# A block of two layers in float32: the low part of every fourth weight unit, made by an adding transfer instead of a VectorE subtraction

## The chip, the core and the metric

The kernel runs on one core of a Trainium2 chip. The metric is the device time of one execution in microseconds (us). A core has five engines with instruction queues of their own: TensorE (PE, matrix products; its weight loads are listed as PEld), VectorE (DVE), ScalarE (ACT), GpSimd (POOL) and SyncE (SP, which here only issues transfers). Each queue is worked off in order; engines wait for each other by semaphores. Transfers between HBM and SBUF run on 16 DMA engines beside all that; they can be issued from the queues of SP, ACT and POOL.

## What is computed

The reference takes x (256 tokens by 2048) through two layers, each a mixer and an MLP, with a root-mean-square norm ahead and a residual sum behind each:

```python
for layer in range(DEPTH):                     # DEPTH = 2
    j = layer // 2
    if layer % 2 == 0:
        y = s5_hgrn2_layer(rms_norm(h, even_norm[j]), even_w_in[j], ...)
    else:
        y = attention_layer(rms_norm(h, odd_norm[j]), odd_w_qkv[j], ...)
    h = h + y
    h = h + squared_relu_mlp(rms_norm(h, mlp_norm[layer]), mlp_w_up[layer], mlp_w_down[layer])
```

The first mixer is a state-space scan and a gated recurrence side by side, the second attention over a sliding window. An MLP is `square(relu(x @ w_up)) @ w_down` with 8192 hidden columns. Nearly all of the work is products of 256 tokens with weights: 2048x5120, 1024x1024 and 2048x2048 in the first mixer, 2048x2560 and 2048x2048 in the second, 2048x8192 and 8192x2048 in each MLP. All of it is float32.

## The kernel before, in words

**Products in parts.** TensorE is fed with float32r, a rounded form of float32. To keep float32's precision, each operand is split into a high part (the value rounded to float32r) and a low part (value minus high part), and three products are summed: high x high, high x low and low x high. The activations are kept as such pairs (class `Pair`), and every weight is split on its way in.

**Units.** All weights are cut, in the order of their use, into 704 units of 512 KB: 128 partitions by 1024 float32, as `nk` row blocks of 128 by `1024 // nk` columns (two blocks of 512 columns; four of 256 for the MLP's up product). In order: 80 units of the first projection, 8 of a gate, 32 of the first output product, 256 of the first MLP, 40 and 32 of the attention, 256 of the second MLP. For each unit:

- `emit_dma` (L92 to L98) issues the load into a tile `raw` from SP's queue (L97). There are four raw tiles.
- `emit_split` (L100 to L107) makes the high part `whi` by an ACT copy that rounds (L105), and the low part `wlo` by a DVE subtraction, raw minus high (L106). There are four tiles of each. Only unit 0 is handled in two pieces.
- `wblock`, `ublock` and `xblock` (L138 to L185) use the unit: 12 to 24 products through the helper `mm` (L136), of which a third read `wlo`. They gather a block of the result in PSUM over several units. In `xblock` the weights are the moving operand, in the other two the stationary one.

**How far ahead.** `advance` (L109 to L119) is called by the blocks for each unit: before unit i is used, the loads up to unit i + 6 and the splits up to unit i + 3 are emitted, a load never more than four units ahead of the splits. So a split must wait until the unit before last has left its tiles, and a load until the raw tile of four units ago has been read.

**Other work.** The mixers are generators put on a list `side`; after each unit `pump` lets them emit a little. They use all engines. On POOL's queue lie, before the change, only some memsets, small powers for the norms (L348, L770, L878, L984), small loads at the start and the load of h (L847).

**Order.** The order of the instructions in each queue is settled when the kernel is built: a scheduler takes the emitted instructions by priority, times them in a simulation of its own, and gives tiles to buffers as it goes (`schedule_with_timeline_sim=True`). Semaphore waits follow from which instruction reads or writes which tile. The MLP's stages run up, up, down, up, down, up, down, down over quarters of the hidden columns (L931 to L938).

Of the kernel before, what the change touches and what calls it, by code (L numbers as in the profile page):

```python
# [8 lines left out]
F32 = mybir.dt.float32  # L9
# [4 lines left out]
AF = mybir.ActivationFunctionType  # L14
ALU = mybir.AluOpType
# [45 lines left out]
def hybrid_kernel(ctx: ExitStack, tc: tile.TileContext, x, even_norm, even_w_in, s5_lambda_re, s5_lambda_im,  # L61
                  s5_log_dt, s5_b_re, s5_b_im, s5_c_re, s5_c_im, s5_d, s5_w_glu, s5_b_glu, hgrn_lower_bound,
                  hgrn_o_norm, even_w_out, odd_norm, odd_w_qkv, q_norm, k_norm, att_sinks, odd_w_out,
                  mlp_norm, mlp_w_up, mlp_w_down, cfd, cmd, out, stop=None):
    nc = tc.nc
    V, S, G, PE = nc.vector, nc.scalar, nc.gpsimd, nc.tensor
# [20 lines left out]
    def pieces(i):  # L87

        nk = units[i][3]
        return [slice(k, k + 1) for k in range(nk)] if i == 0 else [slice(0, nk)]  # L90
# [9 lines left out]
    def emit_split(i):  # L100
        raw, nk = raws.pop(i), units[i][3]
        hi = wp.tile([P, nk, 1024 // nk], F32R, tag="whi", name="whi")
        lo = wp.tile([P, nk, 1024 // nk], F32R, tag="wlo", name="wlo")
        for ks in pieces(i):
            S.copy(out=hi[:, ks], in_=raw[:, ks])  # L105
            V.tensor_tensor(out=lo[:, ks], in0=raw[:, ks], in1=hi[:, ks].bitcast(F32), op=ALU.subtract)  # L106
        splits[i] = (hi, lo)  # L107

    def advance():  # L109
        i = ptr["use"]  # L110
        while ptr["dma"] < min(len(units), i + LOOK_DMA + 1) or ptr["split"] < min(len(units), i + LOOK + 1):
            if ptr["dma"] < min(len(units), i + LOOK_DMA + 1) and ptr["dma"] < ptr["split"] + 4:
                emit_dma(ptr["dma"])
                ptr["dma"] += 1
            else:
                emit_split(ptr["split"])
                ptr["split"] += 1
        ptr["use"] += 1
        return splits.pop(i)  # L119
# [193 lines left out]
    for q in range(8):  # L313
        lastx = make_xT(xt, XT0, "g0", 2 * q, 2)
        if q == 0:
            with tc.issue_after(lastx[2].ins):
                for _ in range(REWARM):
                    PE.matmul(wps, warm[:, 0:P], warm, start=True, stop=True, skip_group_check=True)
        if q < 4:
            emit_split(ptr["split"])  # L320
            ptr["split"] += 1
            if q < 3:
                emit_dma(ptr["dma"])
                ptr["dma"] += 1
                load_x(5 + q)
# [818 lines left out]
```

## Time and profile before

| | |
|---|---|
| median of 3 runs | 2093.21 us (2092.36 to 2093.96) |
| the profiled execution | 2093.33 us, of which the span of the program's instructions 2091.4 us |
| mean granted TensorE clock | 0.998 of full speed |
| the two MLPs, from the timeline | about 410 to 1130 us and 1383 to 2091 us |
| HBM read and written | 374.75 MB and 2.10 MB |
| transfers issued from POOL's queue (q0) | 672 packets, 2.15 MB |

How to read it: a row of instructions names the source line, engine, operation and tiles (written <- read), then the count, the busy time and the mean duration, then the idle time of the engine ahead of them and what ended it. A row of the waits names who waited for whom, the total in us, how often, and the longest. A row of the timeline has the start and the duration first. A row of transfers has the queue that issues them, their count and size, and the median time from issue to landing. "acc" is a block's sum in PSUM, "chi" and "clo" the pair of the MLP's hidden activations (and scratch elsewhere), "x" the pair of a norm's output, "h" the residual stream, "m" the mixers' PSUM tiles.

### The profile page before, as it was taken

The page shows a single profiled execution, that of the slowest core. Times are in us where ns is not written, and L with a number is a line of the kernel's source. Part 1 is how long each engine was busy: PE and PEld are TensorE (multiplying, and loading weights), DVE is VectorE, ACT ScalarE, POOL GpSimd, SP SyncE. Part 2 cuts the span into 40 slices and gives each one's busy share as a digit, 9 for nine tenths or more (in the row PEclk, how much of TensorE's full clock was granted, in tenths as well). Part 3 has the DMA queues.
Part 4 walks back from the last instruction along what each step waited for, and adds up shares of the span by engine and source line. Part 5 has one row for each costly group of instructions (what it writes and reads, how often), then busy time and mean ns, then how long its engine had stood idle before and what let it go on. Part 6 is the DMA issues. An engine that isn't in the chain of part 4 may idle for free.

```text
span 2091.4 us, 30709 instructions
## 1 busy us (share of the span) xinstructions
PE 2077.8 (99%) x12208; PEld 1771.9 (85%) x12208; DVE 1319.9 (63%) x1794; ACT 1036.9 (50%) x1385; POOL 37.8 (2%) x38
## 2 busy tenths in 40 slices
PE   9999999999999999999999999999999999999999
PEld 8988988888888888888888888788888888888887
DVE  6799967666655565565555688776564555565554
ACT  5877555454443444444344477554443444344332
POOL 2000000000000000000000110000000000000000
PEclk9999999999999999999999999999999999999999
DMA  8454644556655665665555643466665665665564
GB/s 247 121 152 142 210 151 163 177 177 188 190 191 193 191 190 191 193 190 191 192 190 183 190 149 125 140 181 187 188 190 193 192 190 192 193 190 191 192 205 147
DMA packets 263968, 378.86 MB, mean 181 GB/s; under 512 B 14120, under 2 KB 147792, under 8 KB 263504
## 3 DMA queue, kind: packets, MB, share of 16 engines
q1 hardware_dynamic: 262400, 373.62, 56.9%
q8 instruction: 96, 1.57, 0.3%
q0 software_dynamic: 672, 2.15, 0.3%
q10 hardware_dynamic: 752, 1.12, 0.2%
q14 instruction: 48, 0.39, 0.1%
HBM read 374.75 MB, written 2.10 MB: 180 GB/s over the span
## 4 chain that ended last, share of the span: by engine, by line
PE 97%; DMA 1%; ACT 1%; DVE 0%; issue 0%; DVEq 0%; SPq 0%; ACTq 0%
PE acc L136 92%; PE m L136 4%; DMA raw<-in_even_w_in_dram 1%; PE m L1037 1%; PE m L304 1%; ACT whi L105 0%; PE m L400 0%; PE m L1071 0%; ACT chi L530 0%; PE m L777 0%; DVE wlo L106 0%; DVE t L343 0%; PE m L537 0%; PE m L509 0%; ACT L832 0%
## 5 line engine op out<-in xcount | busy, mean ns | idle before, releaser
L106 DVE TENSOR_TENSOR wlo<-raw,whi 128x1024 fp32r<-128x1024 f32 (+1 forms) x705 | 860.8, 1222 | 685.4 <-ACT whi L105 684.8
L105 ACT CAST whi<-raw 128x1024 fp32r<-128x1024 f32 (+1 forms) x705 | 740.5, 1051 | 964.6 <-PE acc L136 838.9
L136 PE MATMUL acc<-x,whi 128*128 128x512 f32 (+1 forms) x2944 | 811.1, 362 | 2.5 <-ACT x L843 2.4
L136 PEld LDWEIGHTS acc<-x,wlo 128*128 128x128 f32 x2496 | 470.5, 189 | 92.1 <-DVE wlo L106 0.9
L136 PE MATMUL acc<-x,wlo 128*128 128x256 f32 x2496 | 530.5, 279 | 0.7 <-DVE wlo L106 0.7
L136 PE MATMUL acc<-whi,chi 128*128 128x512 f32 x1280 | 499.6, 390 | 0.0
L136 PE MATMUL acc<-whi,clo 128*128 128x512 f32 x1280 | 499.2, 390 | 0.0
L136 PE MATMUL acc<-wlo,chi 128*128 128x512 f32 x1280 | 498.6, 390 | 0.0
L136 PEld LDWEIGHTS acc<-x,whi 128*128 128x128 f32 x2944 | 453.9, 190 | 4.8 <-ACT x L843 2.8
L136 PEld LDWEIGHTS acc<-whi,chi 128*128 128x128 f32 x1280 | 240.3, 188 | 50.3 <-issue 0.8
L136 PEld LDWEIGHTS acc<-whi,clo 128*128 128x128 f32 x1280 | 240.3, 188 | 49.3
L136 PEld LDWEIGHTS acc<-wlo,chi 128*128 128x128 f32 x1280 | 240.3, 188 | 49.1
L136 PE MATMUL acc<-whi,x 128*128 128x512 f32 x576 | 181.5, 393 | 0.0
L136 PEld LDWEIGHTS acc<-whi,x 128*128 128x128 f32 x576 | 107.5, 188 | 22.4 <-issue 0.4
L136 PE MATMUL acc<-wlo,x 128*128 128x512 f32 x288 | 113.3, 394 | 0.0
L136 PEld LDWEIGHTS acc<-wlo,x 128*128 128x128 f32 x288 | 54.1, 188 | 10.8 <-issue 0.2
L926 DVE SCALAR_TENSOR_TENSOR h<-acc,rs2g,h 128x512 f32<-128x512 f32 x64 | 45.1, 747 | 21.3 <-PE acc L136 21.3
L912 DVE SCALAR_TENSOR_TENSOR t<-t 128x512 f32<-128x512 f32 x64 | 44.3, 693 | 2.2
L911 DVE TENSOR_TENSOR t<-acc,t 128x512 f32<-128x512 f32 x64 | 43.8, 684 | 0.0
L915 DVE TENSOR_TENSOR clo<-t,chi 128x512 fp32r<-128x512 f32 x64 | 43.8, 684 | 0.0
L914 ACT CAST chi<-t 128x512 fp32r<-128x512 f32 x64 | 39.4, 616 | 0.0
L910 ACT COPY t<-acc 128x512 f32<-128x512 f32 x64 | 37.1, 579 | 0.0
(213 smaller groups left out, 899.9 us busy)
## 6 DMA issues: line engine op xcount, KB each, us to landing
raw<-in_mlp_w_up_dram SPq DMA_DIRECT2D x256, 512.0 KB, 3.7
raw<-in_mlp_w_down_dram SPq DMA_DIRECT2D x256, 512.0 KB, 3.6
raw<-in_even_w_in_dram SPq DMA_DIRECT2D x79, 512.0 KB, 3.9
raw<-in_odd_w_qkv_dram SPq DMA_DIRECT2D x40, 512.0 KB, 3.7
raw<-in_even_w_out_dram SPq DMA_DIRECT2D x32, 512.0 KB, 3.6
raw<-in_odd_w_out_dram SPq DMA_DIRECT2D x32, 512.0 KB, 3.7
raw<-in_s_w_glu_dram SPq DMA_DIRECT2D x8, 512.0 KB, 3.5
xt<-in_x_dram SPq DMA_DIRECT2D x8, 256.0 KB, 8.0
```

The source lines that it names most:

```text
L105: S.copy(out=hi[:, ks], in_=raw[:, ks])
L106: V.tensor_tensor(out=lo[:, ks], in0=raw[:, ks], in1=hi[:, ks].bitcast(F32), op=ALU.subtract)
L136: PE.matmul(o, a, b, start=start, stop=stop, skip_group_check=True, **kw)
L304: ipe = PE.transpose(ps[:, b, t * P:(t + 1) * P], src[:, t, (a + b) * P:(a + b + 1) * P], ident)
L910: S.copy(out=r, in_=acc[:, :, 1])
L911: V.tensor_tensor(out=r, in0=acc[:, :, 0], in1=r, op=ALU.add)
L912: V.scalar_tensor_tensor(out=r, in0=r, scalar=0.0, in1=r, op0=ALU.max, op1=ALU.mult)
L914: S.copy(out=ch[c].hi[:, ks, :], in_=r)
L915: V.tensor_tensor(out=ch[c].lo[:, ks, :], in0=r, in1=ch[c].hi[:, ks, :].bitcast(F32), op=ALU.subtract)
L926: V.scalar_tensor_tensor(out=h[:, t, cs], in0=acc[:, t], scalar=norm.rs2[:, t:t + 1], in1=h[:, t, cs], op0=ALU.mult, op1=ALU.add)
L1037: PE.transpose(ps[:, r, a, :], pr[:, 2 * a + r, k * P:(k + 1) * P], ident)
```

## The change

For every unit i with i % 4 == 3 and i > 11 the DVE subtraction is left out. A second ACT pass writes the negated high part into `lo`, and a transfer issued from POOL's queue adds the raw weights to what stands in `lo`. The result is again raw minus high. All other units are split as before.

```diff
         for ks in pieces(i):
             S.copy(out=hi[:, ks], in_=raw[:, ks])
+            if i % 4 == 3 and i > 11:
+
+                S.activation(out=lo[:, ks], in_=hi[:, ks].bitcast(F32), func=AF.Copy, scale=-1.0)
+                G.dma_start(out=lo[:, ks], in_=raw[:, ks], accum_op=ALU.add)
+                continue
             V.tensor_tensor(out=lo[:, ks], in0=raw[:, ks], in1=hi[:, ks].bitcast(F32), op=ALU.subtract)
         splits[i] = (hi, lo)
```

Here `S` is ACT, `V` is DVE and `G` is POOL; `ks` is the whole unit for all units but the first.

## The prediction

> **What bounds the kernel now.** I read the page's totals first, then the chain that ended last, then the waits of TensorE.
>
> ```profile
> span 2091.4 us, 30709 instructions
> PE 2077.8 (99%) x12208; PEld 1771.9 (85%) x12208; DVE 1319.9 (63%) x1794; ACT 1036.9 (50%) x1385; POOL 37.8 (2%) x38
> PE 97%; DMA 1%; ACT 1%; DVE 0%; issue 0%; DVEq 0%; SPq 0%; ACTq 0%
> ```
>
> The profiled execution took 2093.33 us, 1.9 us of it around the span of 2091.4 us; the median of the runs is 2093.21 us, so the two agree to 0.01% and I count from 2093.3. TensorE (PE) is busy in 99% of the span and carries 97% of the chain. VectorE (DVE), which the change relieves, has 0% of the chain and is idle for more than a third of the time. The waits of TensorE say what a faster low part could give:
>
> ```profile
> PE acc L136 <- ACT x L843: 2.4, 1, 2.4
> PE acc L136 <- DVE wlo L106: 0.7, 1, 0.7
> PEld acc L136 <- DVE wlo L106: 0.9, 1, 0.9
> PEld m L1037 <- DVE wlo L106: 0.4, 1, 0.4
> PEld m L136 <- DVE wlo L106: 0.4, 1, 0.4
> ```
>
> The columns are total us, times, longest. In the whole kernel TensorE and its weight loads wait for the DVE subtraction four times, 2.4 us together. So the change can win at most about 0.1%, and the question is what it can lose: how late a low part may come, and how late the DMA makes it.
>
> How much slack is there? ScalarE's (ACT) casts of four consecutive units and the next, in an MLP down stage, and two of the subtractions behind them:
>
> ```profile
> 1001.23 1.06 ACT L105 CAST whi<-raw 128x1024 fp32r<-128x1024 f32 x1 [1.67 <-PE acc L136]
> 1003.95 1.05 ACT L105 CAST whi<-raw 128x1024 fp32r<-128x1024 f32 x1 [1.66 <-PE acc L136]
> 1006.67 1.05 ACT L105 CAST whi<-raw 128x1024 fp32r<-128x1024 f32 x1 [1.67 <-PE acc L136]
> 1009.39 1.05 ACT L105 CAST whi<-raw 128x1024 fp32r<-128x1024 f32 x1 [1.67 <-PE acc L136]
> 1012.11 1.05 ACT L105 CAST whi<-raw 128x1024 fp32r<-128x1024 f32 x1 [1.67 <-PE acc L136]
> 1005.04 1.22 DVE L106 TENSOR_TENSOR wlo<-raw,whi 128x1024 fp32r<-128x1024 f32 x1 [1.26 <-ACT whi L105]
> ```
>
> First column start, second duration. One unit passes every 2.72 us here, and every cast is released by TensorE finishing a unit: the split of unit i+3 starts when unit i-1 leaves its buffer, so the high and low parts have three units of time to be ready. The DVE starts 0.04 us after the cast ends (1003.95 + 1.05 = 5.00, then 5.04). By stage, with the casts counted (microseconds, busy, count, clock, DMA share, GB/s):
>
> ```profile
> 0.00:410.00 410.00, 125.28 (x121) 0.99 0.55 170
> 410.00:1130.00 720.00, 273.36 (x260) 1.00 0.60 189
> 1130.00:1383.00 253.00, 77.72 (x75) 1.00 0.50 156
> 1383.00:2091.00 708.00, 265.41 (x252) 1.00 0.59 188
> ```
>
> Rows two and four are the two MLPs: 720/260 = 2.77 us a unit, 11.08 us for four units. Elsewhere, where TensorE also does the mixers' work, four units take 410/121 x 4 = 13.55 and 253/75 x 4 = 13.49 us.
>
> **The change part by part.** There are 704 units (the 512 KB loads below, two 256 KB pieces making one unit); those with i % 4 = 3 and i > 11 are 15, 19, ... 703, in all 173. Each MLP has 256 units, so 64 of them, together 128; 45 lie elsewhere.
>
> ```profile
> L106 DVE TENSOR_TENSOR wlo<-raw,whi 128x1024 fp32r<-128x1024 f32 (+1 forms) x705 | 860.8, 1222 | 685.4 <-ACT whi L105 684.8
> raw<-in_mlp_w_up_dram SPq DMA_DIRECT2D x256, 512.0 KB, 3.7
> raw<-in_mlp_w_down_dram SPq DMA_DIRECT2D x256, 512.0 KB, 3.6
> raw<-in_even_w_in_dram SPq DMA_DIRECT2D x79, 512.0 KB, 3.9
> h<-in_x_dram POOLq DMA_DIRECT2D x2, 1024.0 KB, 8.7
> t<-in_k_norm_dram POOLq DMA_DIRECT2D x2, 0.2 KB, 5.0
> q1 hardware_dynamic: 262400, 373.62, 56.9%
> ```
>
> *Removed:* 173 DVE subtractions of 1.222 us, 211 us of DVE time, none of it on the path: worth 0 to 2.4 us (the waits above). *Added on ACT:* 173 passes that write the negated high part, same shape as the cast, so 1.05 us each, 182 us. ACT's share goes from 50% to about 58%; the cover is the 1.67 us of idle time ahead of each cast, and 0.6 us of it is left. If that cover is gone (where ACT also evicts), the next cast is late by under 1 us against three units of lead: nothing. I take 0 for it by itself; it counts below, since the pass delays the transfer.
>
> *Added on GpSimd's queue:* 173 transfers of 512 KB from raw into lo that add. No row shows an adding transfer, or one from SBUF to SBUF, so I bound the time from issue to landing, A. Data: the loads moved 373.62 MB in 56.9% of 2091.4 us, so the engines move 314 KB per us while busy; 0.524 MB take 1.67 us if counted once, 3.34 us if the engines pay for reading both operands. Fixed part: the two h transfers lie in the middle of the kernel, on this queue, over 128 partitions, beside weight loads; 2.1 MB at 314 KB/us are 6.7 us of their 8.7, which leaves 2.0. The smallest transfer on this queue, at the kernel's start, has practically no data and took 5.0. So A lies between 2.0 + 1.67 = 3.7 and 5.0 + 3.3 = 8.3 us; the h row taken whole, 8.7, is the upper end I keep. An addition must read two operands, so I count the data twice; of the fixed part I take 3.2, nearer to h (its place and shape) than to the tiny one. A = 6.5 us.
>
> The Trainium skill (Collectives: The Full Stack, section "The bandwidth ceiling") says that a DMA addition is half as fast as a copy because each chunk needs two read descriptors on one ring, not because adding costs time; no run here shows it yet. By that page 3.34 us would be the data part, by a copy's price 1.67 us, and the sum below would drop to A = 4.9 us, which is just hidden.
>
> *What waits for the transfer.* First, the raw tile. It has four buffers, and the subtraction used to free it 2.3 us after the cast began. SyncE's queue shows what that sets off:
>
> ```profile
> SPq L97 <- DVE wlo L106: 1585.8, 646, 10.0
> ACT whi L105 <- PE acc L136: 838.9, 516, 3.1
> ACT whi L105 <- DMA raw<-in_even_w_in_dram: 9.7, 8, 2.1
> ```
>
> 646 of the loads sit at the head of SyncE's queue waiting for a subtraction to free a raw tile; the casts wait for a load only 8 times, all in the first stage. Units with i % 4 = 3 use every fourth raw tile; if the tiles are handed out in turn it is always the same one, and its loop is: load 3.7, cast 1.05, negation 1.05, transfer A, and about five handovers of 0.04 = 0.2. That is 6.0 + A for every four units, against 11.08 in the MLPs. It closes without loss only for A up to 5.1 us. Today's loop is 3.7 + 1.05 + 1.22 + 0.1 = 6.1, five microseconds of slack. With A = 6.5 the loop is 12.5: 1.42 us lost per four units, 128 x 1.42 = 182 us. In the other stages 12.5 is under 13.5: 0. Behind the waiting load on SyncE's queue stand the loads of the next three units, in order; they have the same five microseconds of slack and are released in a burst, so they are not late next, but they share the engines with the adding transfer, which is one more reason not to take A at its low end.
>
> Second, the low part itself: from the split's release to its use are three units, 8.3 us in the MLPs, less 2.1 for the two ACT passes and 0.1 for handovers: A up to 6.1, or 6.3 where a first product with the high part covers 0.2. At A = 6.5 this loop alone would lose 0.2 to 0.4 us; the raw loop is longer and covers it.
>
> Third, GpSimd's queue, which is in order: the few powers and memsets of the mixers and norms can stand behind a transfer that waits for ACT's two passes, about 2 us each, and a transfer can stand behind a memset that waits for TensorE:
>
> ```profile
> POOL t L670 <- PE m L136: 238.0, 2, 188.3
> ```
>
> Two such waits could cost a few us each in the first stage, 0 to 10 us in all; I take 0. DMA load: 128 transfers of 3.34 us of engine time over 1428 us raise the share in the MLPs from 0.60 by 0.30 to about 0.9, still under 1.
>
> Sum: 2093.3 - 0 + 0 + 182 = about 2275 us.
>
> **The rivals.** *Hidden anyway (the other side): not slower.* The place is the raw tile's loop, the deciding point A = 5.1 us. With the fixed part of the h rows and the data once or twice A is 3.7 to 5.3, and then nothing is late; TensorE goes on as before, 2092 us. For it: the only mid-kernel rows of this queue. Against: the 5.0 us of tiny transfers, and engines that are 60% busy already. Chance 0.25. The Trainium skill (DMA: Bandwidth & Descriptors, section "Anatomy of one DMA — SWDGE (gpsimd) path") gives a fit for this path, 2.0 us plus the bytes at 436 KB per us: an estimate of 3.2 us for 512 KB, 4.4 if both reads count, hence this rival's time. The trace doesn't quite agree: by the fit the two h transfers together should land in 6.8 us, and took 8.7.
>
> *The low part is late, the raw tile isn't.* If the raw tiles go out as they come free, the next load takes another tile, and only the second loop is left, from A = 6.2 us on: at 6.5 it costs 0.3 x 128 = 38 us, at 7.5 166 us, so about 2130 to 2260 us. Nothing in the trace of before tells in which order tiles are handed out, since there they come free in turn. Chance 0.13.
>
> *The adding transfer is far slower than any row.* If the addition itself is slow, or the engines saturate, A exceeds 8.7 us: the loop is over 14.7, 3.62 x 128 + 1.2 x 45 = 517 us, so 2610 us and more. Against: nothing but the distance to the rows. Chance 0.11.
>
> *Faster.* The 2.4 us of waits for DVE and a reordering that happens to help: 2088 us at best. Chance 0.03.
>
> **How the numbers follow.** A measurement of this kernel can tell about 0.2%, 4 us, from no change. The forecast, the raw tile's loop with A between 5.1 and 8.7 us, has 0.48 and is likeliest at 2275 us; its own range is 2097 to 2610. Hidden 0.25, low part alone 0.13, far slower 0.11, faster 0.03. The cases of both signs hold much, so the range reaches down to the hidden case with what it may win, 2088, and up to the forecast's end, 2610; beyond it lies the far slower case. Faster 0.03; same 0.23 (hidden, less a little for stalls behind GpSimd's memsets); slower 0.74.
>
> **What would show each step.** Right: 173 adding transfers on GpSimd's queue, 6 to 7 us to landing; DVE's L106 falls by 173 and 211 us; 173 new ACT passes of about 1.05 us; SyncE's loads wait for the adding transfer; the casts wait for loads of the MLP weights, which they don't now; TensorE's waits, in the MLPs alone, sum to some 180 us at about 1.4 us per four units; the DMA share rises toward 0.9. Wrong: A under 5 us and no new TensorE waits (hidden); waits of TensorE for the low part while casts still wait for TensorE and not for loads (the second loop); or losses also in the stages outside the MLPs (A far over 8).

## The result, and the profile after

The changed kernel takes 2272.35 us (median of four runs, 2271.38 to 2276.61), the kernel before, on the same chip, 2093.01 us: 1.0861 times as long, 95% interval 1.0847 to 1.0875. That is 179 us slower. The page of the changed kernel's profile, the lines that answer to those shown of before:

```profile
span 2270.0 us, 31253 instructions
PE 2145.8 (95%) x12208; PEld 1804.1 (79%) x12208; DVE 1118.1 (49%) x1621; ACT 1198.2 (53%) x1558; POOL 186.6 (8%) x211
q1 hardware_dynamic: 262400, 373.62, 50.3%
q0 software_dynamic: 25584, 92.87, 22.3%
L108 ACT ACTIVATE wlo<-whi 128x1024 fp32r<-128x1024 f32 x173 | 183.4, 1060 | 2.8 <-ACT whi L105 0.2
raw<-in_mlp_w_up_dram SPq DMA_DIRECT2D x256, 512.0 KB, 5.0
raw<-in_mlp_w_down_dram SPq DMA_DIRECT2D x256, 512.0 KB, 4.6
wlo<-raw POOLq DMA_DIRECT2D x173, 512.0 KB, 4.9
```

DVE is relieved by 202 us, ACT does 173 passes more, and the packets of GpSimd's queue (q0) now take 22.3% of the DMA engines' time. The new transfer needs 4.9 us from issue to landing, and the weight loads about a microsecond more than before. TensorE's share falls from 99% to 95%. Its waits, the casts' waits and SyncE's waits for the new transfer (total us, times, longest):

```profile
PE acc L141 <- DMA wlo<-raw: 105.6, 48, 3.5
ACT whi L105 <- PE acc L141: 863.1, 464, 7.8
ACT whi L105 <- DMA raw<-in_mlp_w_up_dram: 65.2, 26, 5.0
SPq L97 <- DMA wlo<-raw: 637.7, 171, 12.1
```

TensorE waits for the adding transfer 48 times, 105.6 us in all, where it waited for DVE for less than a microsecond. 25 of these waits last 3.1 to 3.5 us and make 85 of the 105.6 us. SyncE's loads now wait for the transfer to free a raw tile, as forecast; but the casts still wait for TensorE nearly always and for loads seldom, so it is not the raw tile that is missing. And TensorE is slow for a while after a wait. One stall in an MLP down stage, from the timeline, the start and the duration first:

```profile
1119.04 0.39 PE L141 MATMUL acc<-whi,chi 128*128 128x512 f32 x1
1122.91 0.50 PE L141 MATMUL acc<-wlo,chi 128*128 128x512 f32 x1 [3.48 <-DMA wlo<-raw]
1123.24 0.49 PE L141 MATMUL acc<-whi,clo 128*128 128x512 f32 x1
1123.53 0.63 PE L141 MATMUL acc<-whi,chi 128*128 128x512 f32 x1
```

The first product with the unit's low part comes 3.48 us late, and then a product takes 0.63 us instead of 0.39. By stretches (length, PE, PEld, DVE, ACT and POOL busy, granted clock, DMA share, GB/s): the 3.4 us behind the stall before this one, the time between the two, and the 3.5 us behind this one:

```profile
1095.80:1099.20 3.40, 3.40 (x9) 2.67 (x10) 0.00 (x0) 0.00 (x0) 0.00 (x0) 0.54 0.73 239
1099.20:1122.90 23.70, 20.23 (x89) 16.41 (x87) 8.76 (x8) 10.34 (x10) 2.65 (x3) 0.99 0.67 189
1122.90:1126.40 3.50, 3.49 (x9) 2.77 (x10) 0.00 (x0) 0.00 (x0) 0.00 (x0) 0.57 0.76 238
```

For some 3.4 us behind these stalls the granted clock is about half. That holds for 20 of the 25 waits over 3 us; behind three the clock was at half for some 6 us, behind two not at all. Over the span it is 0.976, before 0.998: 2270 x 0.024 less 2091 x 0.002 are 50 us of lost clock. Waits of 105.6 and clock of 50 make 156 of the 179 us; what the other 23 are is not shown. By stage the two MLPs lost 80 and 68 us (from the first to the last product of their 256 units: 708.7 to 788.8, and 706.0 to 773.7), most of it in the down stages, where 32 units went from 87.1 to some 103 us; an up stage of 32 units lost about two. The other 31 us were lost outside the MLPs, 13.7 of them in waits for the transfer.

The two stalls lie 27.1 us apart. Eight units take 21.8 us, and the rest is the loss: in the middle of a down stage every second one of the changed units stalls, the other does not. What ACT and GpSimd did for the two kinds, i % 8 = 3 (it stalls at 1122.91 above) and then i % 8 = 7:

```profile
1108.36 1.05 ACT L105 CAST whi<-raw 128x1024 fp32r<-128x1024 f32 x1 [1.67 <-PE acc L141]
1112.93 2.00 ACT L105 CAST whi<-raw 128x1024 fp32r<-128x1024 f32 x2 [3.52 <-PE acc L141]
1114.84 1.06 ACT L108 ACTIVATE wlo<-whi 128x1024 fp32r<-128x1024 f32 x1
1116.19 0.85 POOL L109 DMA_DIRECT2D wlo<-raw  x1 [2.49 <-ACT wlo L108]
1116.22 0.37 SPq L97 DMA_DIRECT2D raw<-in_mlp_w_down_dram  x1
...
1127.37 1.05 ACT L105 CAST whi<-raw 128x1024 fp32r<-128x1024 f32 x1 [7.09 <-PE acc L141]
1128.44 1.06 ACT L108 ACTIVATE wlo<-whi 128x1024 fp32r<-128x1024 f32 x1
1129.80 0.85 POOL L109 DMA_DIRECT2D wlo<-raw  x1 [12.76 <-ACT wlo L108]
```

In the second kind the negation follows its cast and the transfer is issued 2.43 us after the cast began. In the first kind three things are worse. The cast is due one unit (2.72 us) after the one at 1108.36, at 1111.08, but TensorE releases its tile only at 1112.93. Two casts then run in a row (the row with x2): the next unit's cast stands ahead of the negation in ACT's queue. And the transfer, issued 3.26 us after the cast, has a weight load issued 0.03 us behind it (the next unit's subtraction, which ended at 1116.18, released it) and lands after 6.7 us, not 4.8. From the trace's landings, all 39 transfers with a load issued within 0.5 us behind them took 6.5 to 8.1 us, median 6.7; the other 134 had a median of 4.8.

Why TensorE releases the tile late shows in its products just before:

```profile
1108.16 0.61 PE L141 MATMUL acc<-whi,chi 128*128 128x512 f32 x2
...
1112.46 0.62 PE L141 MATMUL acc<-whi,clo 128*128 128x512 f32 x2
1112.92 0.39 PE L141 MATMUL acc<-whi,chi 128*128 128x512 f32 x1
```

The program writes the products of a down unit as high x high, low x high, high x low, over and over. Here, in the changed unit before (i % 8 = 7), two high x high products stand in a row at the start and two high x low ones at 1112.46, in the middle of the next unit: the scheduler has moved products ahead of those with the low part, and a last product with this unit's high tile is left behind. The cast that needs the tile starts behind it, 1.85 us late. Presumably its simulation has the low part come late; no run shows it.

So the theory after the result is not the forecast's: **the low part lands too late, because the order in the queues ate the lead**; the rival is the forecast's own, **the raw tile's loop**.

### The profile page after: what moved, and what is told of

It is laid out like the page before. It is cut to its first block, busy times and chain, and to the rows that moved or that the text cites. A ratio compares the mean times of both kernels' runs of the same rounds, so it can differ in the third digit from the quotient of the medians.

```text
span 2270.0 us, 31253 instructions
## 1 busy us (share of the span) xinstructions
PE 2145.8 (95%) x12208; PEld 1804.1 (79%) x12208; DVE 1118.1 (49%) x1621; ACT 1198.2 (53%) x1558; POOL 186.6 (8%) x211
## 3 DMA queue, kind: packets, MB, share of 16 engines
q0 software_dynamic: 25584, 92.87, 22.3%
## 5 line engine op out<-in xcount | busy, mean ns | idle before, releaser
L111 DVE TENSOR_TENSOR wlo<-raw,whi 128x1024 fp32r<-128x1024 f32 (+1 forms) x532 | 650.0, 1222 | 802.3 <-ACT whi L105 798.6
L141 PE MATMUL acc<-wlo,chi 128*128 128x512 f32 x1280 | 514.8, 405 | 83.7 <-DMA wlo<-raw 83.7
L141 PEld LDWEIGHTS acc<-x,wlo 128*128 128x128 f32 x2496 | 466.1, 189 | 108.9 <-DMA wlo<-raw 21.8
L141 PE MATMUL acc<-whi,chi 128*128 128x512 f32 x1280 | 508.6, 401 | 2.2 <-ACT chi L1055 1.7
L141 PE MATMUL acc<-whi,clo 128*128 128x512 f32 x1280 | 509.8, 402 | 0.0
L141 PEld LDWEIGHTS acc<-x,whi 128*128 128x128 f32 x2944 | 460.4, 191 | 9.0 <-issue 1.4
L141 PEld LDWEIGHTS acc<-wlo,chi 128*128 128x128 f32 x1280 | 248.9, 194 | 149.2 <-DMA wlo<-raw 97.6
L109 POOL DMA_DIRECT2D wlo<-raw x173 | 147.8, 854 | 1962.1 <-ACT wlo L108 1574.7
L141 PEld LDWEIGHTS acc<-whi,chi 128*128 128x128 f32 x1280 | 249.5, 195 | 56.8 <-ACT chi L1055 2.9
L141 PEld LDWEIGHTS acc<-whi,clo 128*128 128x128 f32 x1280 | 249.5, 195 | 51.3
L108 ACT ACTIVATE wlo<-whi 128x1024 fp32r<-128x1024 f32 x173 | 183.4, 1060 | 2.8 <-ACT whi L105 0.2
```

Source lines behind the costliest of these rows:

```text
L108: S.activation(out=lo[:, ks], in_=hi[:, ks].bitcast(F32), func=AF.Copy, scale=-1.0)
L109: G.dma_start(out=lo[:, ks], in_=raw[:, ks], accum_op=ALU.add)
L141: PE.matmul(o, a, b, start=start, stop=stop, skip_group_check=True, **kw)
```

## The experiments

Beside the first eight runs the kernel before took 2093.44 us. Each experiment was timed once, except the version with the transfer in the MLPs alone (ten runs); thirteen runs of the kernel before lie between 2090.06 and 2093.99 us, so differences of a few us in single runs say nothing.

**Without the transfer** (what is left out: the low part is only the negated high part).

```diff
-                G.dma_start(out=lo[:, ks], in_=raw[:, ks], accum_op=ALU.add)
```

> The adding transfer is left out, the second ACT pass stays: the low part of every fourth unit is only the negated high part, so the low x high product of these units is a wrong number and only the time counts. Both the theory of the raw tile's loop (the forecast) and the theory that the low part itself lands too late put the whole loss on the transfer: 2092 to 2100 us, no waits of TensorE for low parts. A third theory, that the ACT pass or the new order of the queues costs the time by itself, expects over 2150 us.

Measured: 2094.07 us, granted clock 1.000, and no wait of TensorE for a low part. The whole loss belongs to the transfer and to the orders that the scheduler chooses with it, none to the ACT pass; and 211 us less of DVE work gain nothing.

**Five raw tiles.**

```diff
-        raw = wp.tile(..., tag="raw", name="raw", bufs=4)
+        raw = wp.tile(..., tag="raw", name="raw", bufs=5)
-            if ... and ptr["dma"] < ptr["split"] + 4:
+            if ... and ptr["dma"] < ptr["split"] + 5:
-LOOK_DMA = 6
+LOOK_DMA = 7
```

and `sp` with `bufs=5` instead of 6.

> The changed kernel with five raw tiles instead of four, loads up to seven units ahead, and one buffer less of the mixers' scratch to pay for it. Raw tile's loop: four units then have 13.85 us instead of 11.08 for a loop of about 10.9 to 12.5 us, the loss is gone, 2092 to 2120 us. Low part late: the wait for the low part does not depend on raw tiles, 2250 to 2290 us with the same waits of TensorE for the transfer in the MLP down stages.

Measured: 2279.47 us, no faster. Its waits:

```profile
PE acc L141 <- DMA wlo<-raw: 117.9, 47, 5.1
ACT whi L105 <- DMA raw<-in_mlp_w_up_dram: 3.0, 2, 1.6
```

The few waits of the casts for MLP loads are gone (65.2 to 3.0 us), and TensorE waits as before. The raw tile's loop is refuted as the cause.

**One more pair of split tiles**, with a raw tile and a scratch buffer less.

```diff
-        hi = wp.tile(..., name="whi")
-        lo = wp.tile(..., name="wlo")
+        hi = wp.tile(..., name="whi", bufs=5)
+        lo = wp.tile(..., name="wlo", bufs=5)
-LOOK = 3
+LOOK = 4
```

with `LOOK_DMA = 7`, raw `bufs=3`, loads three units ahead of the splits, `sp` with `bufs=5`.

> The changed kernel with five pairs of high and low tiles instead of four and splits four units ahead instead of three, paid for with one raw tile (three instead of four) and one scratch buffer. Low part late: one unit more of lead, 2.7 us, takes most of each 3.4 us stall away, 2095 to 2150 us. Raw tile's loop: with a raw tile fewer the loop is shorter of time than before, 2272 us or more, and the casts wait for loads.

Measured: 2241.43 us, clock 0.995. Neither fits. Its casts wait for loads:

```profile
ACT whi L105 <- DMA raw<-in_mlp_w_down_dram: 394.3, 140, 5.8
ACT whi L105 <- DMA raw<-in_mlp_w_up_dram: 303.6, 136, 7.0
PE acc L141 <- DMA wlo<-raw: 94.9, 115, 3.7
```

With three raw tiles the loop of the forecast does become the bound: four units of the MLPs take 12.0 us (769.7 and 770.2 us for the 256), and a changed unit there needs 11.9 us at the median from the issue of its load to the landing of its transfer. It spreads the waits: 115 short ones of 0.8 us in place of 48 of 2.2, after which the clock hardly falls. Several things were changed at once, so this run says little on the extra lead; that a loop of the raw tile would show in the casts' rows, it shows well.

**The negation first**, straight from the raw weights.

```diff
-            S.copy(out=hi[:, ks], in_=raw[:, ks])
             if i % 4 == 3 and i > 11:
-                S.activation(out=lo[:, ks], in_=hi[:, ks].bitcast(F32), func=AF.Copy, scale=-1.0)
+                S.activation(out=lo[:, ks], in_=raw[:, ks], func=AF.Copy, scale=-1.0)
                 G.dma_start(out=lo[:, ks], in_=raw[:, ks], accum_op=ALU.add)
+                S.copy(out=hi[:, ks], in_=raw[:, ks])
                 continue
+            S.copy(out=hi[:, ks], in_=raw[:, ks])
```

> ACT writes the negated high part straight from the raw weights, ahead of the cast, so that the transfer can be issued one to two us sooner; nothing else changes. Low part late: the stalls of 3.4 us in the MLP down stages shrink to about 1.5 to 2.4 us, 2150 to 2210 us, and fewer of them are long enough to slow the clock. Raw tile's loop: it is 1.05 us shorter, which would give back up to 128 x 1.05 = 134 us, 2140 us; the two are told apart by who waits: in the first TensorE for the transfer, in the second the casts for loads.

Measured: 2126.23 us, clock 0.998; TensorE's waits for the transfer fall from 105.6 to 19.2 us. Most of the loss is undone, more than either range allowed; by the time alone the run is nearer to the 2140 us of the raw tile's loop. What tells the two apart are the waits: TensorE's fell by 86 us, while ACT's passes wait for MLP loads longer than before, 211.5 us against 68.4, most of it now ahead of the negation. Waiting for raw tiles grew and the time fell, so the raw tile is not what cost it. The sooner issue is not all that changed: none of the 173 transfers has a load issued within 0.5 us behind it any more, against 39.

**What the transfer costs**, in two runs. First a copy in place of the addition (the low part is then the raw weight):

```diff
-                G.dma_start(out=lo[:, ks], in_=raw[:, ks], accum_op=ALU.add)
+                G.dma_start(out=lo[:, ks], in_=raw[:, ks])
```

> The transfer copies the raw weights into the low tile instead of adding them, so the low part of every fourth unit is the whole weight, a wrong number; waits and bytes written are the same. If the addition (two operands read, or the adding itself) is what makes the transfer take 4.8 to 6.7 us, it falls to 3.5 us or less and the time to 2095 to 2150 us. If the fixed cost of a transfer from GpSimd's queue is most of it, it stays at 4 to 4.8 us and the time at 2200 to 2270 us.

Measured: 2185.29 us, between the two ranges; the transfer itself is as short as the first expects.

```profile
wlo<-raw POOLq DMA_DIRECT2D x173, 512.0 KB, 3.0
q0 software_dynamic: 25584, 92.87, 11.9%
```

A copy of the same tile takes 3.0 us, the addition 4.9, and the engines' share (11.9% of 2183 us against 22.3% of 2270) is 1.5 us a transfer against 2.9: the addition takes twice the copy's engine time, as counting both operands has it. The run does not part the second reading from the adding. The order of the queues is the changed kernel's, and the stalls remain, 2.3 us each at the median in the down units with i % 8 = 3, where the copy takes 5.5 us beside its load. Second, the transfers in full, but into a scratch tile that nobody reads, beside all DVE subtractions (shortened):

```diff
+        if i % 4 == 3 and i > 11:
+            G.dma_start(out=scr, in_=raw, accum_op=ALU.add)
```

> The kernel before, with all DVE subtractions, and besides the same 173 adding transfers from the raw tiles into a scratch tile that nobody reads (one buffer of the mixers' scratch less). Low part late: nobody waits for these transfers, so 2092 to 2105 us, although they hold the raw tiles and load the DMA engines as before. Raw tile's loop or contention among transfers: a loss of 50 us or more remains, with casts waiting for loads.

Measured: 2100.98 us, clock 0.997.

```profile
scr<-raw POOLq DMA_DIRECT2D x173, 512.0 KB, 6.2
ACT whi L105 <- DMA raw<-in_mlp_w_down_dram: 99.0, 46, 7.7
440.00:1130.00 690.00, 690.00 (x3517) 586.89 (x3516) 391.62 (x388) 303.18 (x338) 53.61 (x63) 1.00 0.84 237
```

The DMA engines are 84% busy in the first MLP, the transfer takes 6.2 us, and TensorE is busy without a gap there. The casts do wait for down loads, 46 times, but most of this hides behind the lead: of the 7.5 us, some 6.5 lie in the last 64 down units, which take 180.7 us against 174.3. Holding the raw tiles and loading the engines costs at most 7.5 us; nearly the whole loss is TensorE waiting for the low part.

**Both orders pinned.** ACT's negation right behind its cast, and TensorE's products of the three block routines as the program writes them (shortened):

```diff
-            S.copy(out=hi[:, ks], in_=raw[:, ks])
+            if (i - 1) % 4 == 3 and neg is not None:
+                with tc.issue_after(neg.ins):
+                    S.copy(out=hi[:, ks], in_=raw[:, ks])
+            else:
+                S.copy(out=hi[:, ks], in_=raw[:, ks])
...
+    def mmo(*a):
+        with tc.issue_after(lastmm.ins):
+            lastmm = mm(*a)
```

> The changed kernel with two orders pinned as the code writes them: the negation right behind its cast (not behind the next unit's cast), and the products of the three block routines in program order. If the 3.4 us stalls come from these two reorderings (1.9 us of a late cast and 0.8 us of a late negation in every second of these units, together with the loads that then run beside the transfer), the stalls in the down stages shrink under 1 us: 2095 to 2150 us. If the transfer is too long by itself, 2230 us or more.

Measured: 2114.65 us, clock 0.996. ACT and GpSimd in a down stage:

```profile
1012.14 1.06 ACT L109 CAST whi<-raw 128x1024 fp32r<-128x1024 f32 x1 [1.71 <-PE acc L147]
1013.23 1.06 ACT L112 ACTIVATE wlo<-whi 128x1024 fp32r<-128x1024 f32 x1
1014.58 0.85 POOL L113 DMA_DIRECT2D wlo<-raw  x1 [10.03 <-ACT wlo L112]
1014.82 1.05 ACT L107 CAST whi<-raw 128x1024 fp32r<-128x1024 f32 x1 [0.53 <-PE acc L147]
```

In the down stages the transfer is now issued 2.44 us after the cast in both kinds of units (medians; 2.8 in the up stages), and it lands 4.8 us later, 0.9 us ahead of its use. The MLPs take 710.9 and 710.2 us against 708.7 and 706.0 before. 158 of 179 us are back, with every transfer still there.

**Work put into the stalls.** Ten products into an unused PSUM tile ahead of the first low product of the down units with i % 8 = 3 (shortened):

```diff
+                    if t == 0 and kk == 0 and u % 8 == 3 and down:
+                        wm = pm([P, 512])
+                        for _ in range(10):
+                            mm(wm, hi[:, 0, 0:P], hi[:, 0, :], True, True)
```

(pinned in this place with `issue_after`).

> The changed kernel plus ten products into an unused PSUM tile (2.3 us at full clock) ahead of the first product with the low part in the units i % 8 = 3 of the down stages, where TensorE otherwise stands still for 3.4 us. If part of the loss is that TensorE's clock halves for 3.4 us after such a stall (27 stalls, 1.7 us each), the added work makes the kernel faster: 2215 to 2245 us at a granted clock of 0.99. If the clock is not part of it, 2270 us or more.

Measured: 2263.12 us, clock 0.994.

```profile
1114.10 0.39 PE L141 MATMUL acc<-whi,chi 128*128 128x512 f32 x1
1114.32 2.43 PE L141 MATMUL m<-whi 128*128 128x512 f32 x10
1118.05 0.50 PE L141 MATMUL acc<-wlo,chi 128*128 128x512 f32 x1 [1.29 <-DMA wlo<-raw]
1118.38 0.39 PE L141 MATMUL acc<-whi,clo 128*128 128x512 f32 x1
```

320 products more make the kernel 9 us faster: the products behind the stall take 0.39 us again. That the clock falls with long gaps is shown. The gain is 9 us and not the 27 to 57 expected, and the trace tells why. In 23 of the 32 places the ten products lie in a stall, and two such stalls follow each other after some 25.6 us instead of 27.1: 1.5 us won each time, about what a stall was taken to cost in clock, some 35 us in all. In the other nine places no wait follows them, so ten products of 0.23 us are simply added, some 20 us. The down stages take 17 us less together than in the changed kernel, and 8 us are lost elsewhere, which is not explained.

**One order at a time**, with the time of the kernel before at 2091.69 us in these runs. TensorE's order alone:

> The changed kernel with TensorE's products of the three block routines in program order; ACT's order is left to the scheduler. If the late release of the tiles (products with the late low part moved behind products of the next unit, so that the cast four units on starts 1.9 us late) is the larger part of the stalls: 2115 to 2170 us. If ACT's order is: over 2200 us.

Measured: 2119.09 us. ACT's order alone:

> The changed kernel with the negation pinned right behind its cast; TensorE's order is left to the scheduler. It can bring the transfer at most 0.8 to 0.9 us earlier in half of the units: if that is a minor part, 2200 to 2260 us; if it is the larger part (because the transfer then also escapes the loads beside it), under 2170 us.

Measured: 2151.90 us; the transfers in the down units with i % 8 = 3 take 4.8 us instead of 6.7, and the stalls 0.8 us instead of 3.4. So 0.8 us won on ACT is worth 2.6: the negation ahead of the next cast also moves the next unit's subtraction, and with it the load that it releases, behind the transfer. Either order by itself undoes most of the loss, TensorE's 153 us and ACT's 120, together 158: they are not additive, since either alone already ends the long stalls of the down stages.

**The best version of the idea, and a control.** Both orders pinned, and the transfer in the MLPs' units alone (`120 <= i < 376 or i >= 448`):

> Both orders pinned and the adding transfer used in the MLPs' units alone (128 instead of 173). With both orders the MLPs' 256 units took 710.9 and 710.2 us against 708.7 and 706.0 before, and the other stages held the rest of the 21 us. If DVE's relief is worth nothing and the transfer is hidden: 2094 to 2102 us, not faster than before. If the relief is worth anything once the transfer is hidden: under 2090 us.

Measured: 2095.13 us (median of ten runs) against 2091.69, a ratio of 1.0018, interval 1.0009 to 1.0028. Its page:

```profile
PE 2078.2 (99%) x12208; PEld 1770.8 (85%) x12208; DVE 1173.7 (56%) x1666; ACT 1164.7 (56%) x1514; POOL 147.7 (7%) x166
```

128 subtractions less on DVE, TensorE at 99% again, and no gain: it is, if anything, 3 us slower. The kernel before with TensorE's order pinned:

> The kernel before with the products of the three block routines pinned in program order. Pinning by itself neither gains nor loses: 2090 to 2097 us. If it gained over 4 us, part of what the pinned versions win back would not belong to the transfer.

Measured: 2093.43 us, within 0.1% of the kernel before in the same runs. Pinning TensorE's order gains nothing where no low part is late.

## Why the prediction was right in number and wrong in mechanism

**What bounds the kernel, and what the relief is worth: right.** TensorE's 99% and 2.4 us of waits for DVE said that nothing can be won. The run without the transfer (2094.07) and the MLP version (2095.13) show it twice. Removed DVE time (forecast 211 us, measured 860.8 - 650.0 = 210.8) and added ACT time (182, measured 183.4) are as counted, and the ACT pass by itself costs nothing, as taken.

**The price A: the data part right, the fixed part too high.** Forecast 6.5 us, 3.3 of it data read twice and 3.2 fixed. Measured 4.9: the copy's 3.0 us less 1.67 of data leaves 1.3 fixed, and the addition adds 1.9. The nearest row, the two large transfers of h, would have given 5.3; I leaned toward a tiny transfer from the kernel's start, which proved no guide to one in its middle. The Trainium skill (Collectives: The Full Stack, section "The bandwidth ceiling") has the addition of a ReduceScatter at half the rate of a copy for its two reads; 2.9 against 1.5 us of engine time agrees for this addition. The estimates from the fit of the Trainium skill (DMA: Bandwidth & Descriptors, section "Anatomy of one DMA — SWDGE (gpsimd) path"), 3.2 us for a copy and 4.4 with both reads, were nearer than my sum: 3.0 and 4.9 measured.

**The step that failed: "if the tiles are handed out in turn it is always the same one", and with it "With A = 6.5 the loop is 12.5: 1.42 us lost per four units, 128 x 1.42 = 182 us".** Before the change the tiles do go in turn: when the subtraction of unit i ends, the load of unit i + 4 starts, 696 times. In the changed kernel they don't: in the MLPs the load that starts when a transfer lands is that of unit i + 5 or i + 6 in 118 of 126 cases and of i + 4 in 8, so the loop spans five units or more, 13.85 us at least. Had it spanned four, it would not have closed even at the measured A: with loads of 4.6 to 5.0 us, which the forecast took at 3.7, 4.6 + 1.05 + 1.06 + 0.3 + 4.9 is 11.9 us by my estimate, against 11.08. The run with three raw tiles shows that loop: there the transfer frees the tile for unit i + 4 (125 of 127 in the MLPs), and four units take 12.0 us. Why the build hands the four tiles out otherwise is not shown. So the loop was the right kind of sum on a premise that did not hold; five raw tiles changed nothing, and that 182 is near the measured 179 is a coincidence. The losses are not evenly 1.4 us per four units either, but some 5 us per eight in the down stages and little in the up stages; and outside the MLPs, where the forecast took 0, 31 us were lost.

**The rival that came true, for a reason that it did not name.** "The low part is late, the raw tile isn't" is what happened, and its condition, that the next load takes another raw tile, held as well. By its own arithmetic, late from A = 6.1 on, an A of 4.9 would have been hidden, and in half of the units it was. In the other half the lead was spent by the queues. For the unit that stalls at 1122.91, counted from 1111.08, when its tiles should have been free: 1.85 us until TensorE lets go of the high tile, 1.91 from the cast to the negation (1.05 expected), 1.06 for the negation, 0.29 of handover to GpSimd (0.04 taken), 6.7 for the transfer beside a load: 11.8 us, where 8.2 were to be had (until 1119.27, when the product behind the one at 1119.04 is due). 3.6 late, against 3.5 measured. I had named the queues (ACT's, SyncE's, GpSimd's) and taken each as if the emitted order stood; a scheduler that times a slow transfer in its own simulation also moves what waits for it, and what waits behind that.

**The clock: not foreseen.** That a stall costs more than its length was in none of the cases. The Trainium skill (TensorE: Matmul & The Clock Gate, section "Part 1: The HAM clock gate (the "warmup" mystery)") states that the array runs at half its clock by default and is released by about 3.4 us of activity; the trace agrees in the main, a granted 0.54 to 0.57 for 3.4 us behind stalls of 3.4 to 3.5 us (two of 25 stalls over 3 us had none), while stalls of 0.8 us (in the runs with five split tiles and with ACT's order pinned) left the clock of the whole span at 0.994 or above.

**GpSimd's queue, the DMA share: right as far as they went.** No large loss came from powers and memsets; the share in the MLPs rose from 0.60 to about 0.76, less than the 0.9 forecast, because the kernel is longer and a transfer takes 2.9 us of engine time and not 3.34, and to 0.84 where the kernel is not longer (the transfers that nobody reads).

## What to carry to other kernels

When a step is handed from an engine to a transfer, its result comes later by the transfer's whole latency, and it is the remaining lead of the consumer that decides, not the engine's busy time: add up release, every instruction ahead of the issue, handovers and the transfer beside its neighbours, and compare with the lead. Where a scheduler fixes the order, look first in the new trace at what moved in each queue around the slow step; pinning two orders won back 158 of 179 us here. Check in the trace, too, in which order tiles are handed out before a loop is built on it. And the relief for an engine off the path stayed worth nothing here, even with the transfer hidden.

## What the runs showed of the hardware

- A 512 KB addition from SBUF into SBUF took 4.8 us from issue to landing when no load was issued just behind it, 6.7 us when a weight load was issued within 0.5 us behind it; a copy of the same tile 2.9 and 5.5 us (medians).
- GpSimd's part in an issue was 0.85 us for the addition and 0.53 us for the copy, against 0.37 us of SyncE for a load of the same size, and it began 0.29 us after ACT's end.
- With the DMA engines 84% busy in the first MLP, the kernel was 7.5 us longer in all.
- A gap of 3.1 to 3.5 us on TensorE was followed by 3.4 us or more at half clock in 23 of 25 cases; with ten products of no use in it, the clock stayed full in 22 of 23.
